# A two-layer decoder trunk on one core: the recurrent stage with a written order on ScalarE and VectorE

## The chip, the cores and the metric

The kernel runs on one core of a Trainium2 chip. Its engines are TensorE (PE, with weight loads shown as PEld), VectorE (DVE), ScalarE (ACT), GpSimd (POOL) and SyncE (SP), each with an instruction queue of its own; 16 DMA engines move data for all of them. The metric is the device time of the whole program in microseconds (us); lower is better.

## What is computed

Two layers work on x, 2048 tokens of 1024 channels in float32. Each normalises the rows, runs a mixer, normalises the result and adds it to x. The first mixer, a gated linear recurrence, is the stage that is changed; the second, a retention mixer, is not. Cut to what matters:

```python
def rglru_mixer(h, w_in, conv_w, conv_b, w_a, b_a, w_x, b_x, lam, w_out):
    u = h @ w_in                                  # 1024 -> 2 x 1536
    xb, gate = u[..., :D_RNN], u[..., D_RNN:]
    xb = causal_depthwise_conv(xb, conv_w, conv_b)   # 4 taps
    r = jax.nn.sigmoid(block_diagonal(xb, w_a) + b_a)   # 16 blocks of 96
    i = jax.nn.sigmoid(block_diagonal(xb, w_x) + b_x)
    log_a = -C_RG * r * jax.nn.softplus(-lam)
    a = jnp.exp(log_a)
    bt = jnp.sqrt(-jnp.expm1(2.0 * log_a)) * (i * xb)
    hseq = scan(h = a * h + bt)                   # along the tokens
    return (hseq * jax.nn.silu(gate)) @ w_out     # 1536 -> 1024

for layer in range(2):
    h = rms_norm(x, norm_pre[layer])
    o = rglru_mixer(h, ...) if layer == 0 else retention_mixer(h, ...)
    x = x + rms_norm(o, norm_post[layer])
```

## The kernel before

Every float32 product is made of three matmuls: each operand is split into a high part `hi` (ACT copies it into a shorter format) and the remainder `lo` (DVE subtracts), and `PASSES` multiplies hi by hi, hi by lo and lo by hi.

The recurrent stage has 16 steps. Step n works on channel group g = n // 4 (384 of the 1536 channels, three tiles of 128) and token block b = n % 4 (512 tokens). A step has two products of 72 matmuls each from x: `mm` gives the recurrent branch, `mg` the gate branch. Between them PE runs the 24 gate products `gt` of the step before (`Tail.products`, in four banks that sigmoids on ACT empty). x comes channel-major in four pieces of a token block. In g = 0 a piece is loaded raw (`xr<-xT`), multiplied by the norm's gain and split (`x_piece`), and stored by a GpSimd DMA to DRAM (`xs`); from g = 1 on it is read back whole (`xp<-xs`). Six weight tiles serve a group; spare buffers hold two more, the others are refilled as the products of b = 3 release theirs.

The norm's row factor is applied after the product: `row_stats` loads the token rows of a block (4 loads), squares them on ACT with a sum, takes a reciprocal root on DVE, and `row_scale` spreads it with four small products (`rbc`) into `sc`. DVE multiplies each product by `sc` (`rglru_u` for `mm`, `Tail.gate` for `mg`), runs the convolution (`Tail.conv`) and splits its result. The rows from 96 up of the three tiles go through a fourth tile `xd` (GpSimd DMAs); its gates `rd` come back by DMAs on ACT's queue into `ri`. The rest of a tail is `tanh`, `exp`, square root (ACT), and in `finish` the decay, the input term, the scan (DVE) and two multiplications on GpSimd, then a store to `y0`. Its ACT functions belong to four groups, so that ACT loads a table (`ACT_TABLE_LOAD`) four times in a step.

Then `out0` multiplies `y0` by the output weights (12 chunks, 72 matmuls for 128 tokens), the products named `o`; the first calls `upto(t, k)` take tokens 0 to 511 over the first chunks.

Order: PE's is the order of the program text. SP's loads and the ACT instructions marked with `keep_in_program_order` also keep it. All else on ACT, DVE and POOL is placed by a planner at compile time from its own costs, so that it can stand earlier or later than in the text. On the chip each engine runs its list in order, and an instruction that waits holds up all behind it. PSUM has eight banks, in turn for all products.

Of the kernel before, what the change touches and what calls it, by code (L numbers as in the profile page):

```python
# [65 lines left out]

class Kernel:
    def __init__(self, nc, tc, ctx, weights):
        self.nc, self.tc, self.ctx = nc, tc, ctx
        self.n = 0  # L70
# [31 lines left out]
    def tiny(self, s, n=1, bufs=4):  # L102
        return self.const.tile([P, n], F32, tag=f"{s}{n}", name=self.uid(s), bufs=bufs)
# [39 lines left out]
    def rsqrt(self, out, z, n=1):  # L143

        v = self.nc.vector
# [68 lines left out]
    def rglru(self, x, xT, gain, conv_w, conv_b, gate_w, b_a, b_x, lam, y0):  # L214


        nc = self.nc
        pool = self.p1 = Pool(self, "p1", (("c", (P, TB), F32, 18), ("ri", (P, 2 * TB), F32, 4),
                                           ("c2", (P, 2 * TB), F32R, 4),
                                           ("gw", (96, 768), F32R, 2), ("dg", (P, P), F32, 2), ("sc", (P, TB), F32, NB),  # L220
# [18 lines left out]
        w, xp = [], []  # L239
        for i in range(6):  # L240
# [4 lines left out]
            w.append(self.weight(shape=(P, KC, P), keep=False, ahead=0))  # L245
            if i < 4:
                xp.append(self.x_piece(0))
        stats = [self.row_stats(x, 0, "c2")]
        gw = gates(0)
        stats.append(self.row_stats(x, 1, "ri"))  # L250
        kt, ke = self.decay_coeffs(lam, pool)
        sc = [pool.tile("sc", (P, TB)) for _ in range(NB)]
        self.fetch_x(2)
        early, tail = [], None
        for n, (g, b) in enumerate(steps):
            final = n + 1 == len(steps)
# [11 lines left out]
            if n > 0:  # L268
                mg = self.rglru_gemm(w[3:], xp, False, (lambda: rows(2, 3)) if n == 1 else None)
            if final:  # L270
                px.close()
                self.py = Pool(self, "p2y", (("yp", (P, 1024), F32R, 8), ("yr", (P, 1024), F32, 2), ("pad", (P, 24), F32, 1)), "right")
                self.yraw = []
                self.ysrc = [(y0[b], 4 * m, o) for b in range(NB) for o in (0, 256) for m in range(3)]
# [16 lines left out]
            if tail:  # L291
                tail.exp()
                tail.finish()
            tail, xp = nxt, new
            if b == 3:
                early.append(self.weight())
                w = [[t.rearrange("p (k c) -> p k c", c=P) for t in e] for e in early]
            if n == 0:
                stats += [self.row_stats(x, i, "ri") for i in (2, 3)]
            if b == 0 and n > 0:  # L300
                gw = tail.gw = gates(g)

        self.fetch_y(2)
# [21 lines left out]
    def x_piece(self, ahead):  # L325
# [714 lines left out]
```

## Time and profile before

| | us |
|---|---|
| median of 3 runs (2703.66 to 2708.68) | 2705.45 |
| the profiled execution | 2711.98 |
| its span in the trace | 2710.2 |
| recurrent stage: first matmul to end of the last `mg` | 7.57 to 679.1 |

The profile is of one execution. Times in its rows count from the start of the span. Busy time is the time that an engine had an instruction in work; idle time is named with the instruction whose end released it. PEclk is the share of full speed that TensorE's clock was granted, 1.00 being 2.4 GHz and 0.50 being 1.2 GHz.

### The profile page before, as it was taken

What the parts mean: (1) busy time and instruction counts of PE and PEld (TensorE: products, weight loads), DVE (VectorE), ACT (ScalarE), POOL (GpSimd) and SP (SyncE); (2) the same over time, 40 slices, a digit from 0 to 9 for tenths busy, and PEclk for the clock granted to TensorE, in tenths of its full rate; (3) what the DMA queues carried; (4) which work ended last, traced back from release to release, by engine and by line L of the source; (5) the groups of instructions that cost most, each with busy time, mean ns of one, the idle gap of its engine ahead of it and who ended that gap; (6) DMA issues with size and microseconds to landing.
All of it is one profiled execution on the core that took longest, in us unless ns stands there. A gap on an engine that the chain in (4) does not pass through costs nothing.

```text
span 2710.2 us, 34140 instructions
## 1 busy us (share of the span) xinstructions
PE 2627.7 (97%) x13224; PEld 2219.1 (82%) x13224; DVE 1567.5 (58%) x3528; ACT 979.6 (36%) x1577; POOL 308.3 (11%) x298
## 2 busy tenths in 40 slices
PE   7889999999899999999999999999999999899998
PEld 6667878878688878888888888888888888778887
DVE  6677777678665555455654556545565456532332
ACT  5545555555432232223422234222342223311110
POOL 1233434345210000000000000000000000000000
PEclk9889999999899999999999999999999999999999
DMA  7554554554554451101411014110141101442231
GB/s 297 202 189 150 175 177 144 181 183 148 161 182 136 141 171 48 55 28 36 141 55 55 28 36 141 55 55 28 36 141 55 55 28 51 148 132 93 93 99 50
DMA packets 90723, 296.81 MB, mean 110 GB/s; under 512 B 10800, under 2 KB 31808, under 8 KB 82368
## 3 DMA queue, kind: packets, MB, share of 16 engines
q1 hardware_dynamic: 68128, 210.93, 24.3%
q0 software_dynamic: 19984, 77.13, 7.6%
q10 hardware_dynamic: 2448, 6.56, 1.0%
q8 instruction: 104, 1.70, 0.3%
q14 instruction: 59, 0.48, 0.1%
HBM read 210.69 MB, written 71.30 MB: 104 GB/s over the span
## 4 chain that ended last, share of the span: by engine, by line
PE 87%; DVE 5%; DMA 4%; ACT 3%; issue 1%; SPq 0%; DVEq 0%; ACTq 0%
PE o L94 26%; PE mm L94 14%; PE v L94 13%; PE g L94 12%; PE k L94 7%; PE q L94 7%; PE st L94 3%; PE gt L94 2%; DMA wraw<-w_in 2%; PE s L94 1%; PE y L97 1%; DVE w L123 1%; DMA wraw<-w_out 1%; DVE c L755 1%; DMA c<-x 1%
## 5 line engine op out<-in xcount | busy, mean ns | idle before, releaser
L94 PE MATMUL mm<-xp,w 128*128 128x512 f32 x2304 | 541.3, 396 | 23.9 <-ACT xp L339 7.6
L94 PEld LDWEIGHTS mm<-xp,w 128*128 128x128 f32 x2304 | 440.6, 192 | 121.6 <-ACT xp L339 7.6
L94 PE MATMUL o<-w,yp 128*128 128x512 f32 x1776 | 417.7, 395 | 10.9 <-ACT w L122 5.0
L94 PEld LDWEIGHTS o<-w,yp 128*128 128x128 f32 x1776 | 336.9, 191 | 83.8 <-ACT w L122 5.5
L94 PE MATMUL g<-w,hp 128*128 128x512 f32 x1536 | 363.6, 392 | 2.9 <-DVE w L123 2.9
L94 PE MATMUL v<-w,hp 128*128 128x512 f32 x1536 | 362.3, 395 | 4.1 <-DVE w L123 3.8
L94 PEld LDWEIGHTS v<-w,hp 128*128 128x128 f32 x1536 | 288.9, 190 | 64.7 <-DVE w L123 4.1
L94 PEld LDWEIGHTS g<-w,hp 128*128 128x128 f32 x1536 | 285.6, 188 | 62.5 <-DVE w L123 4.1
L915 DVE BATCH_NORM_STATS2 bst<-o 128x6 f32<-128x512 f32 x64 | 44.7, 699 | 304.8 <-PE o L94 304.7
L94 PE MATMUL q<-hp,w 128*128 128x256 f32 x1536 | 198.9, 286 | 0.0
L94 PE MATMUL k<-hp,w 128*128 128x256 f32 x1536 | 194.4, 283 | 0.0
L94 PEld LDWEIGHTS k<-hp,w 128*128 128x128 f32 x1536 | 190.7, 192 | 2.4
L94 PEld LDWEIGHTS q<-hp,w 128*128 128x128 f32 x1536 | 187.6, 191 | 0.1
L953 POOL DMA_DIRECT2D y<-m x32 | 21.6, 675 | 1325.7 <-ACT m L931 1325.7
L123 DVE TENSOR_TENSOR w<-wraw,w 128x1024 fp32r<-128x1024 f32 x89 | 114.9, 1301 | 77.7 <-ACT w L122 77.1
L94 PE MATMUL o<-w,w 128*128 128x512 f32 x624 | 144.9, 390 | 1.4 <-ACT w L122 0.9
L94 PEld LDWEIGHTS o<-w,w 128*128 128x128 f32 x624 | 116.9, 188 | 26.5 <-ACT w L122 1.4
L122 ACT ACTIVATE w<-wraw 128x1024 fp32r<-128x1024 f32 x89 | 92.7, 1053 | 114.4 <-DMA wraw<-w_in 88.2
L122 ACT ACTIVATE m<-m 128x128 fp32r<-128x128 f32 (+1 forms) x184 | 91.7, 515 | 112.3 <-DVE mv L916 97.6
L123 DVE TENSOR_TENSOR hp<-hr,hp 128x512 fp32r<-128x512 f32 x128 | 88.4, 693 | 62.2 <-ACT hp L122 40.0
L759 POOL TENSOR_TENSOR c<-c,c 128x512 f32<-128x512 f32 x48 | 91.1, 1902 | 267.4 <-DVE c L755 258.9
L94 PE MATMUL gt<-c,gw 96*96 96x512 f32 x384 | 97.9, 410 | 20.4 <-ACT ri L717 20.4
(179 smaller groups left out, 3324.8 us busy)
## 6 DMA issues: line engine op xcount, KB each, us to landing
xp<-xs SPq DMA_DIRECT2D x48, 1024.0 KB, 5.6
wraw<-w_in SPq DMA_DIRECT2D x66, 512.0 KB, 4.1
hr<-h1T SPq DMA_DIRECT2D x64, 512.0 KB, 4.8
yr<-y SPq DMA_DIRECT2D x52, 512.0 KB, 3.9
xs<-xp POOLq DMA_DIRECT2D x16, 1024.0 KB, 8.8
m<-x SPq DMA_DIRECT2D x32, 512.0 KB, 4.3
y<-m POOLq DMA_DIRECT2D x32, 512.0 KB, 6.1
y<-c POOLq DMA_DIRECT2D x48, 256.0 KB, 2.5
```

Of the source, the lines that this page charges most:

```text
L94: self.pe(self.nc.tensor.matmul(out, lhsT, rhs, start=start, stop=stop))
L97: self.pe(self.nc.tensor.transpose(out, src, self.ident))
L122: self.kept(self.nc.scalar.activation(hi, raw, AF.Copy), keep)
L123: self.kept(self.nc.vector.tensor_tensor(lo, raw, hi.bitcast(F32), ALU.subtract), keep)
L755: nc.vector.tensor_tensor_scan(h, e, s, 0.0 if b == 0 else k.last[j], ALU.mult, ALU.add)
L759: nc.gpsimd.tensor_tensor(sg, h, sg, ALU.mult)
L915: nc.vector.bn_stats(st, bo)
L953: self.nc.gpsimd.dma_start(y1[self.q][:, :, 4 * self.h : 4 * self.h + 4, :], self.sg.rearrange("p c (e t) -> p c e t", t=C))
```

## The change

`Ordered` wraps an engine so that all its instructions keep the order of the text. `va` (DVE) and `aa` (ACT) now issue nearly all of the recurrent stage; only `decay_coeffs` and POOL's instructions stay with the planner. The text is rearranged with it:

- start: the four pieces of the first block are stored by SP (`spill`), not by GpSimd: two behind the rows of block 1, two behind those of block 2. The rows of block 1 are loaded behind those of block 0 and the gate weights; those of blocks 2 and 3 in step 0. Rows 4 to 15 share one reciprocal root of 12 columns (`row_factor`), at the end of step 0. The `rbc` products are moved: block 0 to place 10 of 24 of the first `mg` (was 15), block 1 to place 19 of the second `mm`, blocks 2 and 3 to place 3 of the `mg` of steps 1 and 2.
- each step: the convolution, then its splits (`pieces`), then the weights, tanh, exp, decay, square root, scans with one x piece behind each, and only then the gate branch's `gate` and SiLU, which stood ahead of exp.
- weights: two at b = 1 (was b = 2), four at b = 3, whose raw tiles are all fetched by the end of b = 2 (`fetch(4, px, "xr")`).
- `products` takes the fourth tile first, and SP, not ACT, issues the three DMAs from `rd` to `ri`.
- end: the last `gt` stand behind the first 48 `o` products; in the last step the scans stand ahead of the splits of three of the eight output weights.

```diff
+class Ordered:
+
+    def __getattr__(self, name):
+        f = getattr(self.engine, name)
+
+        def call(*a, **kw):
+            ins = f(*a, **kw)
+            self.tc.keep_in_program_order(ins)
+            return ins
+
+        return call
...
-            self.split(gw[0], gw[1], raw)
+            self.split(gw[0], gw[1], raw, True)
...
-            w.append(self.weight(shape=(P, KC, P), keep=False, ahead=0))
+            w.append(self.weight(shape=(P, KC, P), keep=True, ahead=0))
             if i < 4:
-                xp.append(self.x_piece(0))
...
-        stats = [self.row_stats(x, 0, "c2")]
+                xp.append(self.x_piece(0, spill))
+        rs0, rest = self.tiny("rs", 4), self.tiny("rs", 12)
+        sq0, sqs = self.tiny("sq", 4), self.tiny("sq", 12)
+        stats = [(rs0, 0), (rest, 0), (rest, 4), (rest, 8)]
+        homes = [(self.wpool, "wraw")] * 2 + [(pool, "ri")] * 2
+        self.row_squares(x, 0, [(pool, "c2")] * 4, sq0, 0)
+        self.row_factor(sq0, rs0, 4)
         gw = gates(0)
-        stats.append(self.row_stats(x, 1, "ri"))
+        self.fetch_x(2)
+        self.row_squares(x, 1, homes, sqs, 0)
+        for dst, src in spill[:2]:
+            self.load(dst, src)
         kt, ke = self.decay_coeffs(lam, pool)
         sc = [pool.tile("sc", (P, TB)) for _ in range(NB)]
-        self.fetch_x(2)
...
-            def rows(*bs):
-                for i in bs:
-                    nc.scalar.activation(sc[i], self.row_scale(stats[i]), AF.Copy)
-
-            mm = self.rglru_gemm(w[:3], xp, n == 0, (lambda: rows(1)) if n == 1 else None)
+            def rows(i):
+                return lambda: aa.activation(sc[i], self.row_scale(*stats[i]), AF.Copy)
+
+            mm = self.rglru_gemm(w[:3], xp, n == 0, {19: rows(1)} if n == 1 else {})
             if n == 0:
-                mg = self.rglru_gemm(w[3:], xp, False, lambda: rows(0))
+                mg = self.rglru_gemm(w[3:], xp, False, {10: rows(0)})
             us = self.rglru_u(b, mm, sc[b])
             if tail:
                 tail.products()
             if n > 0:
-                mg = self.rglru_gemm(w[3:], xp, False, (lambda: rows(2, 3)) if n == 1 else None)
...
             nxt = Tail(self, g, b, gw, ba, bx, kt, ke, y0)
             if final:
                 break
             new = []
-            for j in range(3):
-                nxt.conv(j, us[j], cw, cb)
+            if b == 1:
+                self.fetch(2)
+            if n == 0:
+
+                self.row_squares(x, 2, homes, sqs, 4)
+                for dst, src in spill[2:]:
+                    self.load(dst, src)
                 new.append(self.x_piece(2))
-            if b == 2:
-                early = [self.weight() for _ in range(2)]
-            if b == 3:
-                early += [self.weight() for _ in range(3)]
-            if tail:
+                nxt.conv(0, us[0], cw, cb)
+                new.append(self.x_piece(2))
+                self.row_squares(x, 3, homes, sqs, 8)
+                new.append(self.x_piece(2))
+                nxt.gate(mg, sc[b])
+                nxt.conv(1, us[1], cw, cb)
+                new.append(self.x_piece(2))
+                nxt.conv(2, us[2], cw, cb)
+                self.row_factor(sqs, rest, 12)
+                nxt.pieces()
+                nxt.silu()
+            else:
+                for j in range(3):
+                    nxt.conv(j, us[j], cw, cb)
+                nxt.pieces()
+                if b == 1:
+                    early = [self.weight() for _ in range(2)]
+                if b == 3:
+                    early += [self.weight(ahead=0) for _ in range(2)]
                 tail.tanh()
-            new.append(self.x_piece(2))
-            nxt.gate(mg, sc[b])
-            nxt.silu()
-            if tail:
                 tail.exp()
-                tail.finish()
+                if b == 3:
+                    early.append(self.weight(ahead=0))
+                tail.decay()
+                new.append(self.x_piece(2))
+                tail.sqrt()
+                for j in range(3):
+                    tail.scan(j)
+                    new.append(self.x_piece(2))
+                if b == 3:
+                    early.append(self.weight(ahead=0))
+                nxt.gate(mg, sc[b])
+                nxt.silu()
+                if b == 2 and g + 1 < NG:
+                    self.fetch(4, px, "xr")
             tail, xp = nxt, new
             if b == 3:
-                early.append(self.weight())
                 w = [[t.rearrange("p (k c) -> p k c", c=P) for t in e] for e in early]
-            if n == 0:
-                stats += [self.row_stats(x, i, "ri") for i in (2, 3)]
             if b == 0 and n > 0:
                 gw = tail.gw = gates(g)
...
         for j in range(3):
             nxt.conv(j, us[j], cw, cb)
+        nxt.pieces()
+        early += [self.weight() for _ in range(2)]
         tail.tanh()
+        tail.exp()
+        self.pcs = [[self.y_piece(True)]]
+        early.append(self.weight())
+        tail.decay()
+        tail.sqrt()
+        self.pcs[0].append(self.y_piece(True))
+        for j in range(3):
+            tail.scan(j)
         early += [self.weight() for _ in range(2)]
-        tail.exp()
-        tail.finish()
-        self.pcs = [[self.y_piece() for _ in range(2)]]
-        early += [self.weight()]
-        nxt.products()
         nxt.gate(mg, sc[b])
-        self.pcs[0].append(self.y_piece())
-        early += [self.weight() for _ in range(3)]
+        early.append(self.weight())
+        self.pcs[0].append(self.y_piece(True))
         return early, nxt
...
-            self.nc.scalar.activation(hi[:, c], raw[:, c], AF.Copy, scale=gk)
-            self.nc.vector.scalar_tensor_tensor(lo[:, c], raw[:, c], gk, hi[:, c].bitcast(F32), ALU.mult, ALU.subtract)
-        self.nc.gpsimd.dma_start(self.xs[b][j], both.bitcast(F32))
+            self.aa.activation(hi[:, c], raw[:, c], AF.Copy, scale=gk)
+        for c in range(2):
+            k = 2 * j + c
+            gk = self.gain[:, k : k + 1]
+            self.va.scalar_tensor_tensor(lo[:, c], raw[:, c], gk, hi[:, c].bitcast(F32), ALU.mult, ALU.subtract)
+        if later is None:
+            self.nc.gpsimd.dma_start(self.xs[b][j], both.bitcast(F32))
+        else:
+            later.append((self.xs[b][j], both.bitcast(F32)))
         self.fetch_x(ahead)
...
+    def row_squares(self, x, b, homes, sq, at):
+
+        for i, (pool, tag) in enumerate(homes):
+            xn = pool.tile(tag, (P, D))
             self.load(xn, x[b * TB + i * P : b * TB + (i + 1) * P, :])
+            self.aa.activation(xn, xn, AF.Square, accum_out=sq[:, at + i : at + i + 1])
+
+    def row_factor(self, sq, rs, n):
+
+        z = self.tiny("z", n)
+        self.va.tensor_scalar(z, sq, 1.0 / D, RMS_EPS, ALU.mult, ALU.add)
+        self.rsqrt(rs, z, n, self.va)
...
-            if m == 15 and between:
-                between()
+            if m in between:
+                between[m]()
...
+        upto(0, 8)
+        tail.products()
         tail.tanh()
         tail.exp()
+        self.pcs.append([self.y_piece(True)])
+        tail.decay()
+        tail.sqrt()
         tail.silu()
-        self.pcs.append([self.y_piece()])
-        tail.finish()
-        upto(0, 8)
+        for j in range(3):
+            tail.scan(j)
...
+    def pieces(self):
+
+        k = self.k
+        for j in range(3):
+            vp = self.pool.tile("c2", (P, 2, TB), F32R)
+            k.split(vp[:, 0], vp[:, 1], self.xc[j], True)
+            self.nc.gpsimd.dma_start(self.xd[32 * j : 32 * j + 32].bitcast(F32), vp[96:128].bitcast(F32))
+            self.xcp.append(vp)
...
-        for j in range(4):
+        for i, j in enumerate((3, 0, 1, 2)):
             src = self.xd if j == 3 else self.xcp[j][:96]
             dst = rd if j == 3 else ri[j][:96]
             for e, bias in ((0, self.ba), (1, self.bx)):
...
-                self.k.tc.keep_in_program_order(nc.scalar.activation(dst[:, e, :], o, AF.Sigmoid, bias=bias[:, 4 * self.g + j : 4 * self.g + j + 1]))
-        for j in range(3):
-            nc.scalar.dma_start(ri[j][96:128], rd[32 * j : 32 * j + 32])
+                k.aa.activation(dst[:, e, :], o, AF.Sigmoid, bias=bias[:, 4 * self.g + j : 4 * self.g + j + 1])
+            if j == 3:
+                for m in range(3):
+                    k.load(ri[m][96:128], rd[32 * m : 32 * m + 32])
...
+    def decay(self):
+
         for j in range(3):
-            self.k.tc.keep_in_program_order(nc.scalar.activation(self.ri[j][:, 0, :], self.tt[j], AF.Sqrt))
-
-    def finish(self):
+            h, e = self.tt[j], self.ee[j]
+            i = self.ri[j][:, 1, :]
+            self.nc.gpsimd.tensor_tensor(i, i, self.xc[j], ALU.mult)
+            self.k.va.scalar_tensor_tensor(e, e, 1.0, h, ALU.add, ALU.mult)
+            self.k.va.tensor_scalar(e, e, -1.0, 1.0, ALU.mult, ALU.add)
+
+    def sqrt(self):
+        for j in range(3):
+            self.k.aa.activation(self.ri[j][:, 0, :], self.tt[j], AF.Sqrt)
```

## Rows read from the trace of the kernel before

**Rows 1.** the page's busy time of each engine, whole span

```profile
PE 2627.7 (97%) x13224; PEld 2219.1 (82%) x13224; DVE 1567.5 (58%) x3528; ACT 979.6 (36%) x1577; POOL 308.3 (11%) x298
```

**Rows 2.** the chain that ended last, an undisturbed stretch: start, us, what

```profile
263.58 5.55 PE gt L94 x24
269.14 32.66 PE mm L94 x144
```

**Rows 3.** steps b=2,3,0,0: busy us (count) of PE, PEld, DVE, ACT, POOL; clock, DMA

```profile
301.80:340.00 38.20, 38.20 (x169) 30.89 (x169) 29.46 (x47) 21.65 (x29) 17.07 (x12) 1.00 0.53 180
...
340.00:379.30 39.30, 38.33 (x169) 30.68 (x168) 24.97 (x35) 21.96 (x30) 9.83 (x11) 1.00 0.55 187
...
379.30:423.00 43.70, 40.60 (x170) 32.02 (x169) 38.06 (x57) 21.61 (x30) 16.23 (x14) 0.96 0.45 151
...
537.50:581.00 43.50, 40.42 (x170) 31.89 (x169) 38.06 (x57) 21.52 (x30) 16.42 (x14) 0.96 0.48 152
```

**Rows 4.** PE in order of time: start, us, instruction, [idle before, releaser]

```profile
84.44 2.88 PE L94 MATMUL gt<-c,gw 96*96 96x512 f32 x6 [9.47 <-ACT ri L717]
...
177.98 2.88 PE L94 MATMUL gt<-c,gw 96*96 96x512 f32 x6 [8.89 <-ACT ri L717]
...
217.07 5.90 PE L94 MATMUL mm<-xp,w 128*128 128x512 f32 x18 [3.40 <-DMA xp<-xs]
...
232.46 7.77 PE L94 MATMUL mm<-xp,w 128*128 128x512 f32 x33 [2.02 <-DVE w L123]
...
707.58 1.22 PE L94 MATMUL o<-w,yp 128*128 128x512 f32 x2 [5.02 <-ACT w L122]
```

**Rows 5.** busy times of longer stretches, columns as in rows 3

```profile
72.03:90.34 18.31, 8.49 (x26) 5.11 (x24) 12.39 (x41) 13.96 (x25) 0.50 (x1) 0.64 0.65 234
...
90.34:127.93 37.59, 37.03 (x161) 30.30 (x160) 22.15 (x41) 21.04 (x31) 9.33 (x10) 0.95 0.53 185
...
166.14:183.75 17.61, 8.50 (x26) 5.13 (x25) 11.40 (x19) 13.50 (x18) 1.86 (x2) 0.68 0.14 50
...
183.75:222.81 39.06, 35.66 (x145) 28.90 (x144) 26.80 (x38) 20.46 (x27) 10.27 (x10) 0.92 0.57 182
...
222.81:263.58 40.77, 38.75 (x170) 30.85 (x169) 36.55 (x54) 20.32 (x29) 16.00 (x13) 1.00 0.49 162
...
679.10:709.60 30.50, 19.92 (x69) 13.42 (x67) 20.91 (x21) 15.15 (x20) 9.99 (x8) 0.81 0.51 145
...
709.60:757.00 47.40, 47.40 (x198) 38.96 (x199) 32.36 (x60) 20.58 (x30) 9.86 (x9) 0.94 0.51 172
```

**Rows 6.** groups of instructions on DVE and POOL: busy, mean ns, idle before

```profile
L697 DVE SCALAR_TENSOR_TENSOR c<-u,c_cw,c 128x512 f32<-128x512 f32 x144 | 103.9, 775 | 0.0
...
L755 DVE TENSOR_TENSOR_SCAN c<-c,last,ri 128x512 f32<-128x512 f32 x36 | 53.3, 1500 | 0.0
...
L123 DVE TENSOR_TENSOR w<-wraw,w 128x1024 fp32r<-128x1024 f32 x89 | 114.9, 1301 | 77.7 <-ACT w L122 77.1
...
L154 DVE TENSOR_TENSOR rst<-rst,rsz 128x4 f32<-128x4 f32 x12 | 1.9, 162 | 0.4
...
L391 DVE COPY u<-halo 128x3 f32<-128x3 f32 x36 | 27.5, 763 | 0.0
...
L750 POOL TENSOR_TENSOR ri<-ri,c 128x512 f32<-128x512 f32 x48 | 102.5, 2160 | 71.5 <-DMA ri<-ri 63.9 <-issue 7.7
```

**Rows 7.** ACT in order of time, the end of one switch of functions

```profile
175.95 1.28 ACT L717 ACT_TABLE_LOAD   x1
...
177.25 0.68 ACT L717 ACTIVATE ri<-gt,c_ba 96x512 f32<-96x512 f32 x1
```

**Rows 8.** DMA issues (KB, us to landing); busy times of two stretches

```profile
c<-x SPq DMA_DIRECT2D x4, 512.0 KB, 19.1
...
20.00:25.00 5.00, 5.00 (x24) 4.13 (x23) 2.56 (x9) 1.27 (x2) 0.47 (x1) 1.00 1.02 425
...
30.00:35.00 5.00, 5.00 (x24) 4.14 (x23) 0.00 (x0) 3.03 (x5) 0.00 (x0) 1.00 1.04 331
```

More of the change, by code (lines that the diff above doesn't have):

```diff
@@ L102, in tiny @@
     def tiny(self, s, n=1, bufs=4):
-        return self.const.tile([P, n], F32, tag=f"{s}{n}", name=self.uid(s), bufs=bufs)
+        return self.const.tile([P, n], F32, tag=f"{s}{n}", name=self.uid(s), bufs=bufs if n < 12 else 1)
     def bank(self, shape, s="ps"):
@@ L141, in weight, with rsqrt @@
         return hi, lo
-    def rsqrt(self, out, z, n=1):
-        v = self.nc.vector
+    def rsqrt(self, out, z, n=1, v=None):
+        v = v or self.nc.vector
         y, t, zh = self.tiny("rsy", n), self.tiny("rst", n), self.tiny("rsz", n)
@@ L268, in rglru @@
             if n > 0:
-                mg = self.rglru_gemm(w[3:], xp, False, (lambda: rows(2, 3)) if n == 1 else None)
[L270 to L274, printed above, removed]
+                mg = self.rglru_gemm(w[3:], xp, False, {3: rows(n + 1)} if n in (1, 2) else {})
             nxt = Tail(self, g, b, gw, ba, bx, kt, ke, y0)
@@ L300, in rglru @@
             if b == 0 and n > 0:
                 gw = tail.gw = gates(g)
+        px.close()
+        self.py = Pool(self, "p2y", (("yp", (P, 1024), F32R, 8), ("yr", (P, 1024), F32, 2), ("pad", (P, 24), F32, 1)), "right")
+        self.yraw = []
+        self.ysrc = [(y0[b], 4 * m, o) for b in range(NB) for o in (0, 256) for m in range(3)]
         self.fetch_y(2)
@@ L323, in fetch_x, with x_piece @@
             self.xraw.append(raw)
-    def x_piece(self, ahead):
+    def x_piece(self, ahead, later=None):
         g, b, j = self.xnext.pop(0)
@@ L362, in row_scale, with rglru_gemm @@
             dg = self.p1.tile("dg", (P, P))
-            nc.vector.tensor_scalar(dg, self.ident, rs[:, i : i + 1], None, ALU.mult)
+            self.va.tensor_scalar(dg, self.ident, rs[:, at + i : at + i + 1], None, ALU.mult)
             self.mm(rbc[:, i * P : (i + 1) * P], self.ones, dg, start=True, stop=True)
         return rbc
-    def rglru_gemm(self, tiles, xp, arrival=False, between=None):
+    def rglru_gemm(self, tiles, xp, arrival=False, between={}):
         out = [self.bank([P, TB], "mm") for _ in tiles]
@@ L381, in rglru_u @@
     def rglru_u(self, b, mm, scale):
-        nc = self.nc
+        v = self.va
         us = []
@@ L451, in fetch_y, with y_piece @@
             self.yraw.append(raw)
-    def y_piece(self):
+    def y_piece(self, keep=False):
         self.fetch_y(2)
         hi, lo = [self.py.tile("yp", (P, 4, 256), F32R) for _ in range(2)]
-        self.split(hi, lo, self.yraw.pop(0))
+        self.split(hi, lo, self.yraw.pop(0), keep)
         self.fetch_y(2)
@@ L690, in conv @@
     def conv(self, j, u, cw, cb):
[L692 to L695 removed]
+        k, ch = self.k, 3 * self.g + j
+        v = self.pool.tile("c", (P, TB))
+        k.va.tensor_scalar(v, u[:, :TB], cw[:, ch, 0:1], cb[:, ch : ch + 1], ALU.mult, ALU.add)
         for t in range(1, CW):
[L697 to L700 removed]
+            k.va.scalar_tensor_tensor(v, u[:, t : t + TB], cw[:, ch, t : t + 1], v, ALU.mult, ALU.add)
         self.xc.append(v)
[L702 removed]
+    def pieces(self):
[5 more added lines that the diff above has]
+            self.xcp.append(vp)
     def products(self):
@@ new lines, in decay, with scan @@
+            h, e = self.tt[j], self.ee[j]
[6 more added lines that the diff above has]
+            self.k.aa.activation(self.ri[j][:, 0, :], self.tt[j], AF.Sqrt)
+    def scan(self, j):
+        nc, k, b = self.nc, self.k, self.b
+        s, i, h, e, sg = self.ri[j][:, 0, :], self.ri[j][:, 1, :], self.tt[j], self.ee[j], self.sg[j]
+        k.va.scalar_tensor_tensor(s, e, 1.0, s, ALU.add, ALU.mult)
+        k.va.tensor_tensor(s, s, i, ALU.mult)
+        k.va.tensor_tensor_scan(h, e, s, 0.0 if b == 0 else k.last[j], ALU.mult, ALU.add)
+        if b < NB - 1:
+            k.last[j] = k.tiny("last", 1, 6)
+            k.va.tensor_copy(k.last[j], h[:, TB - 1 : TB])
+        nc.gpsimd.tensor_tensor(sg, h, sg, ALU.mult)
+        nc.gpsimd.dma_start(self.y0[b][3 * self.g + j], sg)
```

62 lines of the change are left out of this document (16 added, 46 removed).

## The prediction

> **What bounds the kernel now.** I read the page first. PE is busy for 97% of the span [rows 1], so time can come back only where PE stands or runs at half clock. The chain of waits then gives the floor. In an undisturbed stretch 24 gate products take 5.55 us and 144 branch products 32.66 [rows 2], so a step of the recurrent stage cannot take less than 38.21 us, and one matmul of 512 columns costs 0.227 us. In such a step PE is busy from end to end and DVE for 29.46 us of it [rows 3]: DVE is the next limit, with 8.7 us to spare.
>
> The busy times by stretch show where steps take longer. From the first matmul to the end of the last `mg` 671.5 us pass, where 32 branch products of 16.33 and 15 sets of gates need 605.8. The 66 us over it stand in four places, and a fifth lies behind them.
>
> - Steps 0 to 2, up to 127.93: 120.4 us for five branch products and one set of gates, 87.2. PE stands 9.47 us for a sigmoid queued behind squares of late rows [rows 4], and the gates that follow run at 0.48 us each, half clock [rows 5, 4].
> - Step 3, 166.14 to 222.81: 56.67 us for one step, 18.46 lost. Gates wait 8.89 us for sigmoids that stand on ACT behind a tail whose weights came late; later `mm` waits 3.40 us for an x piece that SP issued behind weight loads [rows 4]. Step 4 loses 40.77 - 38.21 = 2.56 [rows 5], 2.02 of it for the low part of a weight [rows 4].
> - Steps 7 and 8: 39.30 + 43.70 - 76.42 = 6.6 lost [rows 3].
> - Steps 11 and 12 repeat this; the second takes 43.50, 5.3 lost [rows 3].
> - The head of the output product, 679.10 to 757.00: 77.9 us for 24 gates and 240 `o` products, 5.55 + 54.4 = 60.0, so 17.9 lost. 5.02 is a wait for a weight [rows 4]; the clock was 0.81 and 0.94 [rows 5].
>
> **The change part by part.**
>
> *Steps with b = 3.* Today the weights for the next group are fetched by SP between x pieces, so a step 7 leaves DVE idle (24.97 us busy) and step 8 overfull (38.06) [rows 3]. The change fetches all raw tiles a step ahead and splits two weights before tanh, one behind exp, one behind the scans. DVE's work in such a step is the 29.46 of a step with two splits plus two more at 1.23 (1.30 in the mean [rows 6]), 32 us. In the written order DVE waits only for exp, some 3 us, and ends near 35 to 36. Behind it stand SiLU and a table load of 1.28 [rows 7] before the next sigmoids at 38.2 + 0.7. That fits by about 1.5 us. So I recover 17.5 of the 18.46, 2 of the 2.56, 6 of the 6.6 and 4.5 of the 5.3. If the fit fails, each us beyond it costs one per b = 3 step.
>
> The gate's move behind the scans costs nothing while the next gates need only two of its three banks after 2.8 us; it hides behind the 32.66 us of branch products.
>
> *The three DMAs from `rd`* move from ACT to SP and past no queue of loads that waits later than they do: the x loads ahead of them were released when the `mg` before ended, 16 us earlier. The fourth tile's sigmoids come first, so they issue sooner. No gain is counted.
>
> One rule of the Trainium skill weighs against a chain with four switches of function: ScalarE: Activation LUTs, section What ACT_TABLE_LOAD costs, gives 1283 ns for the load and about 1380 ns of draining with it. By it the fit of 1.5 us would be nearly gone and the two switches ahead of the last scans would cost 2.8: a sum smaller by about 4, 2672. The trace has 1.28 us and the sigmoid 0.02 behind [rows 7], so I go by the row.
>
> *The start.* Rows of block 0 take 19.1 us to land behind 4 MB of stores that GpSimd interleaves, with the DMA engines at 1.0 [rows 8]. Deferring the stores leaves 7.3 MB ahead of their end. At 331 to 425 GB/s [rows 8] that is 21 to 25 us instead of 34, and the first `rbc` no longer waits: PE ends step 0 near 43 instead of 48. I take 360, nearer to the lower, in whose stretch GpSimd issues no store.
>
> Then the written order costs. Gate weights, two x pieces, the rows of block 1, two stores and the rows of block 2 make 15.0 MB: block 2 lands near 44, and the first x piece of step 1 stands behind its squares on ACT, so `mm` starts at 46. Behind two more stores and two x pieces block 3 lands near 59 (20.2 MB). Its squares end at 60; behind them stand x piece 3, the gate, two convolutions, x piece 4, the 12-column root (eleven instructions of 0.16 with a start every 0.2 [rows 6]), three low parts and four diagonals: 1.4 + 2.0 + 2.6 + 1.4 + 2.6 + 2.2 + 1.9 + 1.1 = 15.2, at 0.65 to 0.75 for each pass over 512 columns [rows 6]. So the root's `rbc` in the second `mm` can go at 76, after PE has stood since 68. Five places of three matmuls are left, 3.4 us at full and 6.8 at half clock; `mm` ends near 83 (72.03 now), the gates near 88.5, and the second `mg` starts there against 90.34 [rows 5]. Step 1's rest takes 32.7 + 1.4 + 1, to 123.2 instead of 127.93; step 2 pays one more `rbc` (1.4) and 0.7 of DVE pressure: 163.6 instead of 166.14. Gain 2.5. Bounds: if nothing but DMA bounded this part, `mm` would end near 64, 19 us better; if block 3 lands 10 us later, it is 8 us worse than now.
>
> *The end.* PE no longer waits for `gt`'s sigmoids first: 48 `o` products stand ahead. But three output weights are split behind the last scans. Counted from the end of `mg`, DVE does the splits before at about 0, then decay 3, a y piece 1.3, three scans with two multiplications each 8 (scan 1.50 [rows 6]), two weights 2.5, the gate 2; the last weight's load starts when a raw tile frees, at 13, takes some 5 and is split by 20. Work for PE until then is 10.9 us, so 9.5 are lost, with about 3 at half clock after the wait. 12.5 replace 17.9: gain 5. Bounds: 12 if the weights come with the scans, 0 if the last load is 5 us later.
>
> Sum: 2.5 + 17.5 + 2 + 6 + 4.5 + 5 = 37.5 us. The profiled execution took 2711.98, its span 2710.2; it lies 0.24% above the median of 2705.45, so I take the difference from the median: 2668. Past 757.00 nothing is changed, and I expect the same time there.
>
> **The rivals.**
>
> *The start comes out dense.* If block 3's rows land by 50, the chain on DVE is the only limit, step 1 ends 15 to 19 us sooner: 2650. For it: the DMA engines move up to 425 GB/s. Against: the rows are issued behind x loads that wait for DVE.
>
> *The start comes out later.* Rows of block 3 at 70 push everything by 10, since block 1's factor, which needed no other block before, waits for all twelve columns: 2680, with 2 of it hidden. For it: one root for three blocks. Against: fewer stores compete.
>
> *Nothing to win.* If the waits at b = 3 are the DMA engines' own and not the order's, they stay: 2705, within 0.2%. Against: the 3.40 us wait was for an x piece that SP issued late, while DMA share in step 7 is 0.55 [rows 3].
>
> *Slower: DVE and GpSimd cannot run together.* In the 29.46 us step POOL is busy for 17.07, some 13.8 without its six DMA issues. If DVE's back-to-back order leaves POOL no gap, and the two exclude each other, a step takes 29.5 + 13.8 = 43.3, 5.1 over the floor; over 15 steps that is 76 us, less the 37.5: 2744. It decides from 40.7 us of joint work in a step (2.5 over the floor, 15 times). For it: a copy of three columns takes 0.76 us in the mean and POOL's multiplication 2.16 [rows 6], so one does hold up the other. Against: the step of [rows 3] holds 29.46 + 13.8 in 38.20, so the durations already contain the waiting. A milder form, with only the four b = 3 and the two x-splitting steps over, gives +15 and 2683.
>
> The Trainium skill, SBUF — State Buffer, section Who interferes with whom, states that rule: the shared port pair is an exclusive lock, held for a whole instruction. By it 43.3 would be the step; the trace has 38.20.
>
> **How the numbers follow.** My forecast 0.53; dense start 0.14 (2650); later start 0.12 (2680); milder lock 0.10 (2683); nothing won 0.06 (2705); full lock 0.05 (2744). 0.2% is 5.4 us, about what a measurement of this kernel can tell from no change. Faster is everything but the last two: 0.89; within 0.06; slower 0.05. The forecast's own range is 2657 to 2679 from the bounds of its terms. To leave out no more than 2 in 10 I go from 2648, which takes in the dense start, to 2692, which takes in the later start and the milder lock.
>
> **What would show it.** Right: steps 4 to 15 at 38.2 to 39 us with no gap at b = 3 above 1 us; sigmoids never released by DVE's gate; gates near 83 to 89 with PE idle before the `rbc` of the second `mm`; 166.14 becoming about 164 and 222.81 about 203; the output head with one gap on a weight near 9 us. Wrong: a sigmoid of each step released late by SiLU; DVE past 38 us in a step; x or row loads behind stores on SP in step 0; the output weights late beyond 20 us after the last `mg`.

## The result and the profile after

The changed kernel takes 2730.3 us (median of 4 runs, 2723.2 to 2731.1) against 2705.6 before: ratio 1.0084, 95% interval 1.0065 to 1.0104. It is 24.7 us slower, where I had forecast 37.5 faster. The profiled execution has a span of 2729.3 us, 19.1 above that of before, which lay above its own median.

The page's busy times, as in [rows 1]:

```profile
PE 2646.1 (97%) x13224; PEld 2215.4 (81%) x13224; DVE 1598.5 (59%) x3504; ACT 975.0 (36%) x1577; POOL 254.9 (9%) x294
```

PE has the same 13,224 matmuls and stands about as long (83.2 us idle, 82.5 before), but is busy for 18.4 us more. The busy times by stretch, columns as in [rows 3], of steps 6, 8 and 9 and of the output head:

```profile
295.00:334.00 39.00, 39.00 (x170) 31.00 (x169) 30.66 (x45) 19.54 (x27) 11.71 (x12) 1.00 0.51 176
...
373.00:413.40 40.40, 39.27 (x170) 30.95 (x169) 33.12 (x50) 21.33 (x31) 12.56 (x12) 1.00 0.48 156
413.40:456.70 43.30, 41.02 (x170) 31.93 (x169) 32.75 (x48) 22.10 (x30) 11.51 (x12) 0.96 0.52 183
...
679.76:765.80 86.04, 67.44 (x267) 51.16 (x265) 57.15 (x89) 38.46 (x54) 17.93 (x17) 0.90 0.45 147
```

The first is a step without any gap, at a granted clock of 1.00, and takes 39.00 us where [rows 3] has 38.20. So the floor itself moved. PE's instructions in order of time, with what ended the wait before them, can be held against [rows 4]:

```profile
64.61 8.22 PE L112 MATMUL mm<-xp,w 128*128 128x512 f32 x21 [10.77 <-ACT xp L77]
78.96 2.08 PE L112 MATMUL rbc<-dg,ones 128*128 128x128 f32 x8 [6.13 <-DVE dg L77]
...
215.84 3.87 PE L112 MATMUL gt<-c,gw 96*96 96x512 f32 x12 [2.38 <-ACT ri L77]
...
438.33 18.52 PE L112 MATMUL mm<-xp,w 128*128 128x512 f32 x72 [2.24 <-DMA xp<-xs]
...
698.03 4.58 PE L112 MATMUL o<-w,yp 128*128 128x512 f32 x10 [10.64 <-DVE w L141]
...
739.29 4.43 PE L112 MATMUL o<-w,yp 128*128 128x512 f32 x10 [5.48 <-DVE w L141]
```

The waits of 9.47 and 8.89 us for sigmoids are gone. In step 1's first product PE now waits for an x piece and then for the diagonals; `rbc` starts at 78.96, where I had 76. The new waits that were not forecast stand at the gates behind a step with b = 3, at an x piece a step later, and at the second place in the head. The groups on DVE and POOL, columns as in [rows 6] (line 77 is the wrapper that issues all ordered instructions):

```profile
L77 DVE SCALAR_TENSOR_TENSOR c<-u,c_cw,c 128x512 f32<-128x512 f32 x144 | 138.8, 964 | 5.1
...
L77 DVE SCALAR_TENSOR_TENSOR ri<-c,ri 128x512 f32<-128x512 f32 x48 | 54.0, 1126 | 0.0
L77 DVE TENSOR_TENSOR_SCAN c<-c,last,ri 128x512 f32<-128x512 f32 x36 | 46.2, 1284 | 1.3
...
L77 DVE COPY u<-halo 128x3 f32<-128x3 f32 x36 | 5.7, 158 | 0.0
...
L815 POOL TENSOR_TENSOR ri<-ri,c 128x512 f32<-128x512 f32 x48 | 74.4, 1573 | 173.1 <-DMA ri<-ri 115.6 <-ACT ri L77 57.4
```

Before, the scan's first multiplication was

```profile
L753 DVE SCALAR_TENSOR_TENSOR ri<-c,ri 128x512 f32<-128x512 f32 x48 | 32.8, 686 | 8.5 <-ACT ri L743 8.5
```

A convolution's multiply-add takes 964 ns (775 before), the scan's first multiplication 1126 (686 before), while the halo copy fell from 763 to 158 and POOL's multiplication from 2160 to 1573. DVE and POOL in order of time show why:

```profile
278.78 1.81 DVE L77 SCALAR_TENSOR_TENSOR ri<-c,ri 128x512 f32<-128x512 f32 x1
280.70 0.69 DVE L77 TENSOR_TENSOR ri<-ri 128x512 f32<-128x512 f32 x1
...
286.74 1.89 DVE L77 TENSOR_TENSOR c<-mm,sc 128x512 f32<-128x512 f32 x3
...
278.75 1.29 POOL L833 TENSOR_TENSOR c<-c,c 128x512 f32<-128x512 f32 x1 [9.81 <-DVE c L77]
...
286.72 1.29 POOL L833 TENSOR_TENSOR c<-c,c 128x512 f32<-128x512 f32 x1 [1.82 <-DVE c L77]
```

At 278.75 POOL starts to multiply; the DVE instruction issued 0.03 us later takes 1.81 us instead of 0.69. At 286.72 POOL starts again, and three DVE multiplications with one operand in PSUM take 1.89 us together, against 1.87 at 372.47, where POOL does not multiply. The end of step 7, a step with b = 3, on DVE and then on ACT:

```profile
372.47 1.87 DVE L77 TENSOR_TENSOR c<-mm,sc 128x512 f32<-128x512 f32 x3
...
375.02 1.28 ACT L77 ACT_TABLE_LOAD   x1
376.32 0.68 ACT L77 ACTIVATE ri<-gt,c_ba 96x512 f32<-96x512 f32 x1
```

DVE ends the gate at 374.3, 40.3 us after the first gate product of the step. The last SiLU, a table load and only then the sigmoid follow, and the `gt` that started at 372.99 wait 1.13 us for it.

By stretches of the spans (the first two columns are what I forecast and had; the last two are experiments):

| us | forecast | before | changed | e1: place restored | e7: and multiplications on DVE |
|---|---|---|---|---|---|
| to the gates of step 3 | 163.6 | 166.1 | 171.5 | 172.3 | 163.9 |
| step 3 | 39.2 | 56.7 | 39.0 | 38.2 | 38.2 |
| steps 4 to 15, to the last `mg` | 443.8 | 456.3 | 469.2 | 467.7 | 443.0 |
| head, to the first transposes | 72.7 | 77.7 | 85.9 | 84.9 | 88.1 |
| all behind it | 1953.4 | 1953.4 | 1963.6 | 1952.0 | 1953.3 |

### The profile page after: what moved, and what is told of

Read it like the earlier page. It is cut to its first block, busy times and chain, and to the rows that moved or that the text cites. A ratio compares the mean times of both kernels' runs of the same rounds, so it can differ in the third digit from the quotient of the medians.

```text
span 2729.3 us, 34188 instructions
## 1 busy us (share of the span) xinstructions
PE 2646.1 (97%) x13224; PEld 2215.4 (81%) x13224; DVE 1598.5 (59%) x3504; ACT 975.0 (36%) x1577; POOL 254.9 (9%) x294
## 4 chain that ended last, share of the span: by engine, by line
PE 80%; DVE 11%; ACT 3%; DMA 3%; issue 2%; SPq 0%; DVEq 0%; ACTq 0%
PE o L112 26%; PE v L112 13%; PE g L112 12%; PE mm L112 9%; PE k L112 7%; PE q L112 7%; DVE c L77 6%; PE st L112 3%; DVE ri L77 1%; ACT c L77 1%; PE s L112 1%; PE y L115 1%; DVE w L141 1%; PE gt L112 1%; ACT w L140 1%
## 5 line engine op out<-in xcount | busy, mean ns | idle before, releaser
L112 PE MATMUL mm<-xp,w 128*128 128x512 f32 x2304 | 553.5, 401 | 28.6 <-ACT xp L77 18.4
L112 PEld LDWEIGHTS mm<-xp,w 128*128 128x128 f32 x2304 | 440.7, 192 | 137.6 <-ACT xp L77 19.1
L112 PE MATMUL o<-w,yp 128*128 128x512 f32 x1776 | 427.0, 399 | 20.4 <-DVE w L141 17.7
L77 DVE SCALAR_TENSOR_TENSOR c<-u,c_cw,c 128x512 f32<-128x512 f32 x144 | 138.8, 964 | 5.1
L141 DVE TENSOR_TENSOR w<-wraw,w 128x1024 fp32r<-128x1024 f32 x83 | 102.4, 1247 | 45.5 <-ACT w L140 45.0
L473 ACT ACTIVATE m<-o 128x512 f32<-128x512 f32 x62 | 37.0, 597 | 234.0 <-PE o L112 156.0
```

The lines of the kernel that those rows point to most:

```text
L77: ins = f(*a, **kw)
L112: self.pe(self.nc.tensor.matmul(out, lhsT, rhs, start=start, stop=stop))
L141: self.kept(self.nc.vector.tensor_tensor(lo, raw, hi.bitcast(F32), ALU.subtract), keep)
L473: self.kept(nc.scalar.activation(res[:, 512 * i : 512 * i + 512], o[i], AF.Square, accum_out=sq[:, i : i + 1]), keep)
```

## The experiments

**Where the operands lie: e1, e2, e3.** The new 12-column scalars made the constant pool 384 bytes larger by my count of its tiles; no trace shows addresses. All pools filled from the left, the weights among them, moved up by 384 bytes; those filled from the right, with x and y pieces, did not. In the changed kernel the slow products are those with one operand on each side.

```diff
 e1, changed kernel, wpool:      ("pad", (P, 24), F32, 1)  ->  ("pad", (P, 56), F32, 1)
 e2, kernel before, wpool:       ("pad", (P, 24), F32, 1)  ->  ("pad", (P, 120), F32, 1)
 e3, changed kernel, p1x, p2y:   ("pad", (P, 24), F32, 1)  ->  ("pad", (P, 56), F32, 1)
```

> The changed kernel with 128 bytes more of padding ahead of its weights; nothing else differs. The changed kernel's constant pool is 384 bytes larger than before's, so every pool that is filled from the left moved by 384 bytes, and those filled from the right did not; this pad takes the weights back to the place that they had before within a block of 512 bytes. Theory A (a matmul whose two operands lie differently within such a block is slower): 144 branch products take 32.66 us again in place of 33.46, `o` products 0.227 us each in place of 0.232, PE busy goes from 2646 back to about 2628, and the time from 2730 to about 2705 to 2710. Rival B (the order of the work, not the place of its operands, slows PE or makes the whole loss): matmuls stay at 0.2324 us and the time at 2730, within 3 us.

> The kernel before with 384 bytes more of padding ahead of its weights; no instruction and no order differs. Theory A: its branch products take 33.46 us for 144 in place of 32.66, `gt`, `q`, `k`, `g` and `v` keep their rates, PE is busy for about 2646 us, and the time is 2720 to 2730. Rival B: 2705, and 32.66 us for 144.

> The changed kernel with 128 bytes more of padding at the right end of the two pools that hold the x pieces and the y pieces, which moves these pieces 128 bytes down; the weights stay where they slowed. Theory A in its relative form (what counts is how the two operands lie to each other): 32.66 us for 144 products again, and about 2705 to 2712. In its absolute form (the weights' own place counts): 33.46 us, and 2730. Rival B: 2730 and 33.46 us as well.

Measured: e1 2716.2 us (ratio to before 1.0042, 1.0028 to 1.0056), e2 2722.1 (1.0061, 1.0046 to 1.0076), e3 2717.7 in one run. The groups on PE (busy, mean ns; idle and its releasers), first of the changed kernel, then of e1, e2 and e3:

```profile
L112 PE MATMUL mm<-xp,w 128*128 128x512 f32 x2304 | 553.5, 401 | 28.6 <-ACT xp L77 18.4 <-DVE xp L77 4.0 <-DMA xp<-xs 3.9
```

```profile
L112 PE MATMUL mm<-xp,w 128*128 128x512 f32 x2304 | 542.9, 396 | 32.2 <-ACT xp L77 19.5 <-DMA xp<-xs 7.7 <-DVE xp L77 5.0
```

```profile
L94 PE MATMUL mm<-xp,w 128*128 128x512 f32 x2304 | 553.1, 401 | 20.5 <-ACT xp L339 8.1 <-DVE w L123 6.0 <-DVE xp L340 3.7
```

```profile
L112 PE MATMUL mm<-xp,w 128*128 128x512 f32 x2304 | 540.8, 396 | 30.3 <-ACT xp L77 18.3 <-DVE xp L77 4.7 <-DMA xp<-xs 4.4
...
L112 PE MATMUL o<-m,yp 128*128 128x512 f32 x144 | 35.0, 395 | 0.0
```

Theory A holds in its relative form. The kernel before, with not one instruction changed, gets the slow rate from 384 bytes of padding and loses 16.3 us. Moving either operand of the changed kernel by 128 bytes more gives the fast one, with 14.1 us gained in e1; e3's last line is of a later product whose y pool was not moved, and it stays at 35.0 (34.1 in e1, 34.1 before). So weights and pieces that have moved against each other by 0 or by 512 bytes are fast, by 384 slow; other distances were not tried, and with what period the rate returns is not shown. This is 14 of the 24.7 us, and e1 still loses 10.4.

**The x loads behind the weights: e4.** In e1, steps 5, 9 and 13 take 42.7 to 43.0 us. SP's queue and PE in one of them:

```profile
259.88 11.63 SPq L118 DMA_DIRECT2D wraw<-w_in  x4
...
271.57 5.63 SPq L118 DMA_DIRECT2D xp<-xs  x4
...
279.21 18.17 PE L112 MATMUL mm<-xp,w 128*128 128x512 f32 x72 [2.36 <-DMA xp<-xs]
```

```diff
-                    early = [self.weight() for _ in range(2)]
+                    early = [self.weight(ahead=0) for _ in range(2)]
...
                     tail.scan(j)
                     new.append(self.x_piece(2))
+                if b == 1:
+                    self.fetch(2)
```

> On the changed kernel with the 128 bytes of padding (2716.2 us): in the steps with b = 1 the third and fourth raw weight are fetched behind the four x loads instead of ahead of them; no other order changes. Theory C (x loads stand on SP behind two weight loads, which wait for the raw tiles that DVE frees at the low parts of the early weights): the waits of `mm` for an x piece, 2.36, 2.78 and 2.54 us, go, and so does the slower half step behind each, 17.98 to 18.21 us for 72 products in place of 16.4; each of the three steps takes 38.2 us in place of 42.7 to 43.0, and the time falls by 10 to 14, to about 2704. Rival (the DMA engines are busy in that stretch, and the piece lands late anyway): the waits stay within 1 us and the time within 3.

2703.9 us (0.9991, 0.9981 to 1.0001): 12.3 less than e1, as theory C says, and the three waits are gone. The loads did stand behind two weight loads, and those behind DVE's split of the weights. That DVE was late for a reason of its own is seen in e7, where the same waits all but vanish (0.33 us left) without this edit.

**SiLU behind the sigmoids: e5.**

```diff
                 tail.products()
+                if b == 0:
+                    tail.silu()
...
                 nxt.gate(mg, sc[b])
-                nxt.silu()
+                if b < 3:
+                    nxt.silu()
```

> On the same base (2716.2 us): after a step with b = 3 the three SiLUs run behind the sigmoids of the next step instead of ahead of them. Theory D (the gates of that step wait for sigmoids that stand on ACT behind SiLU and a table load, and these behind the gate on DVE, whose work in such a step ends at 40 us): the three waits of `gt` for ACT, 3.06, 1.92 and 1.91 us, go, with the half-clock gates behind them, and the time falls by 8 to 11, to about 2706. Rival (the late place of DVE itself counts, and something else on DVE is late next, the low parts of x or the scales): another wait of 2 to 3 us takes their place, and the time stays within 3 us of 2716.

2710.5 us (1.0018, 1.0008 to 1.0027), 5.7 less, between theory and rival. The gates wait no more (0.21 us left), but part of the gain went back, as the rival said: PE now waits 3.31, 3.99 and 4.52 us for the x piece, 2.36, 2.78 and 2.54 in e1.

```profile
432.65 19.18 PE L112 MATMUL mm<-xp,w 128*128 128x512 f32 x72 [3.99 <-DMA xp<-xs]
```

**The old head: e6.** `tail.products()` stands ahead of `upto(0, 8)` again, and the scans ahead of the last weights and y pieces:

```diff
         for j in range(3):
             tail.scan(j)
-        early += [self.weight() for _ in range(2)]
+        self.pcs = [[self.y_piece(True) for _ in range(2)]]
+        early.append(self.weight())
+        nxt.products()
         nxt.gate(mg, sc[b])
...
```

> On the same base (2716.2 us): the end part alone is undone; the last gate products go ahead of the first output ones again, and the last scans of the tail ahead of the splits of the last output weights. Theory E (the two weights split behind the scans cost more than the cover of 32 products gives): the waits for weights in the head, 11.0 and 5.0 us, become about 5 and 3, and the time falls by about 7, to 2709. Rival (the head is bound by the serial chain of two tails, whatever their order): within 2 us of 2716.

2717.1 us (1.0041, 1.0026 to 1.0056), 0.9 more than e1: the rival. The waits moved: gates 2.96 us, then 4.63 for a weight. The sigmoids of the last tail end at 689.8, but its tanh starts at 706.4, behind two weight copies on ACT that wait for raw tiles, so its scans and the weights behind them are no earlier. So the order of the products alone was not what cost.

**POOL's multiplications on DVE: e7 and e8.** The same two edits, in the changed kernel with e1's padding and (with `nc.vector` for `va`) in the kernel before:

```diff
-            self.nc.gpsimd.tensor_tensor(i, i, self.xc[j], ALU.mult)
+            self.k.va.tensor_tensor(i, i, self.xc[j], ALU.mult)
...
-        nc.gpsimd.tensor_tensor(sg, h, sg, ALU.mult)
+        k.va.tensor_tensor(sg, h, sg, ALU.mult)
```

> On the same base (2716.2 us): both multiplications of a tail that GpSimd does (`ri` by `c`, and `h` by the gate) are done by VectorE, six instructions more a step on DVE and none on POOL but DMA issues. Theory F (a DVE instruction that runs beside a POOL multiplication is held up for about as long as that one runs): a convolution's multiply-add falls from 0.96 us to 0.775 in the mean, the scan's two multiplications from 1.13 and 0.86 to 0.69, and the six new ones cost 0.69 each; DVE is busy for the same time within 1 us a step, and the waits of the steps behind b = 3 stay as they are or shrink: 2710 to 2718. Rival (the durations have another cause, such as PE or ACT reading beside it): durations stay, DVE has 4.1 us more a step, and the steps with b = 3 grow by some 4 us each: 2728 or more.

> The kernel before, with the two multiplications of a tail on VectorE instead of GpSimd; its order and its addresses stay. If the lock between DVE and POOL is what made the written order lose, and the order itself is worth something once the lock is gone: before gains little from this, since its losses in the recurrent stage stand at late weights and squares (9.47, 8.89 and 3.40 us) and not at DVE: 2698 to 2706, well behind the 2688 of the changed kernel with the same edit. Rival (the 28 us came from the lock alone and the written order adds nothing): 2680 to 2690, the same as the changed kernel with that edit.

e7 takes 2688.0 us (0.9935, 0.992 to 0.995): 28.2 less than e1, far below the range I gave. e8 takes 2701.2 (0.9978, 0.9968 to 0.9988), as expected. Groups on DVE in e7, then its step 7 by stretch, the gate on DVE that ends it, and the gate products that follow without a wait:

```profile
L77 DVE SCALAR_TENSOR_TENSOR c<-u,c_cw,c 128x512 f32<-128x512 f32 x144 | 108.3, 752 | 5.1
...
L77 DVE SCALAR_TENSOR_TENSOR ri<-c,ri 128x512 f32<-128x512 f32 x48 | 32.9, 685 | 0.0
...
L77 DVE TENSOR_TENSOR ri<-ri,c 128x512 f32<-128x512 f32 x48 | 32.9, 684 | 0.0
```

```profile
317.00:355.20 38.20, 38.20 (x169) 30.90 (x168) 32.88 (x53) 22.11 (x30) 3.17 (x6) 1.00 0.46 152
```

```profile
352.66 1.88 DVE L77 TENSOR_TENSOR c<-mm,sc 128x512 f32<-128x512 f32 x3
```

```profile
355.22 5.71 PE L112 MATMUL gt<-c,gw 96*96 96x512 f32 x24
```

DVE does 96 multiplications more, some 65.7 us at 0.684, and is busy for 1574.9 us instead of 1598.3: it had been held for 65.7 + 23.4 = 89 us. It was not waiting for POOL's results: in the changed kernel no idle time of PE, DVE or ACT ends on a POOL multiplication. The Trainium skill, SBUF — State Buffer, section Who interferes with whom, says that DVE and GpSimd share a port pair that is locked for a whole instruction, and that a DVE instruction with at most one SBUF input stays out of it unless it runs in a two-port mode; the 1.81 us beside POOL, and the 1.89 for three with a PSUM operand, agree. The first instruction of a convolution, with one SBUF tensor, was held too (784 ns in the mean against 541 in e7); no run here shows its mode.

The kernel before was held about as long: 1567.5 - (1550.3 - 65.6) = 83 us. There it cost only 4.9 us: PE's waits for DVE's splits of weights and x in the recurrent stage (6.0 and 3.8 us) are still there in e8 (6.3 and 3.8). Put together (the changed order with e1's padding):

| us | order of before | written order |
|---|---|---|
| multiplications on POOL | 2705.8 | 2716.2 |
| multiplications on DVE | 2701.2 | 2688.0 |

The written order is worth -13.2 us with the lock gone and +10.4 with it.

**A new head: e9.** On e7, whose head takes 88.1 us:

```diff
-        upto(0, 8)
-        tail.products()
         tail.tanh()
         tail.exp()
-        self.pcs.append([self.y_piece(True)])
-        tail.decay()
         tail.sqrt()
         tail.silu()
-        for j in range(3):
-            tail.scan(j)
+        tail.decay()
+        w.append(self.weight())
+        tail.scan(0)
+        w.append(self.weight())
+        tail.scan(1)
+        tail.scan(2)
+        self.pcs.append([self.y_piece(True)])
+        upto(0, 6)
+        upto(1, 6)
+        upto(0, 8)
         upto(1, 8)
```

and ahead of it, as in e6, scans and `products` before the last weights.

> On the kernel with the multiplications on VectorE (2688.0 us), whose output head takes 88 us from the last `mg` to the first transposes: the scans of the last tail but one and the last gate products go first again, the tanh, exp, sqrt and SiLU of the last tail stand ahead of the last two weights on ACT, its scans between their splits on DVE, and the first two output tiles use six weights each before either waits for the seventh. Theory E2 (the head is the serial chain of two tails, and it stretched because ACT and DVE waited for the raw tiles of the last weights in between): the two waits for weights, 8.8 and 8.1 us, fall to under 3 together, the head takes about 70 us, and the time is about 2670 to 2675. Rival (the DMA of the weights is the limit, whatever the order): the waits return at the seventh and ninth weight with 10 us or more, and the time is 2684 to 2690.

2671.6 us (0.9864, 0.9844 to 0.9884), 16.4 less than e7. The head by stretch, and its longest waits for a weight and a y piece:

```profile
648.50:722.50 74.00, 64.11 (x265) 49.50 (x264) 53.85 (x95) 36.81 (x52) 4.38 (x8) 0.98 0.51 163
```

```profile
680.50 4.16 PE L112 MATMUL o<-w,yp 128*128 128x512 f32 x17 [2.85 <-DVE w L141]
688.38 34.31 PE L112 MATMUL o<-w,yp 128*128 128x512 f32 x143 [3.72 <-DVE yp L141]
```

So the weights' DMA did not bound the head at 88 us. e9 moves the products, the last tail on ACT and DVE, the splits and the places of the `o` products together; e6, with the multiplications still on POOL, says that the products and scans moved without the last tail give nothing. Which share each of the others has was not tried.

**The start: e10, e11, e12.** One root for each block again, and the late rows behind the x pieces; in e10 the core of the edit is

```diff
-                self.row_squares(x, 2, homes, sqs, 4)
...
                 new.append(self.x_piece(2))
-                self.row_squares(x, 3, homes, sqs, 8)
+                xn = self.row_loads(x, 2, homes)
+                nxt.conv(1, us[1], cw, cb)
                 new.append(self.x_piece(2))
...
+                self.row_squares(xn, sqs[2])
+                self.row_factor(sqs[2], rss[2], 4)
                 nxt.silu()
```

with block 3 in step 1 in the same way. It also issues all four stores of the first block behind the rows of block 1 and moves the `rbc` of blocks 2 and 3 from place 3 to 12. No scalar has 12 columns any more, so these kernels need no padding for the fast rate. e11 is e10 with e9's head. e12 is e11 with the x pieces of step 1 put between its convolutions and its weights last.

> On the kernel with the multiplications on VectorE (2688.0 us), start part: each block of rows has its own root again, the rows of block 2 are loaded behind two x loads and squared behind all four x pieces of step 1, the rows of block 3 a step later behind the sigmoids. Theory G (the wait of 10.97 us for ACT is x behind squares of late rows, and the one of 6.90 for the diagonals is the root over twelve columns): both go or fall under 3 us, the first gates start near 72 us in place of 84.3, and the time is about 2675 to 2680. Rival (DMA traffic bounds the start, and the x pieces are late whatever stands ahead of them on ACT): the second `mm` starts at 62 or later, and the time is 2685 to 2690.

> Both edits of the two kernels before this one together, on the kernel with the multiplications on VectorE. By theories E2 and G: about 2660 (2688 less some 16 for the head and 11 for the start). By both rivals: 2684 to 2690.

> On the kernel with the multiplications on VectorE and the new head (2671.6 us), a second form of the start. The first form took the wait of 10.97 us away (gates at 72.5 us instead of 84.3) but lost more in the next step: the x pieces of step 2 stood on ACT behind rows, weights, tanh and exp, and `mm` waited 11.39 us for them. Now the four x pieces of step 2 go between the convolutions and the tail, the last rows are squared between them and behind the scans, the weights of that step come last, and the root of block 2 stands behind the diagonals of block 1. Theory G2 (the order on ACT, and not DMA, bounds the second step too): gates near 70 to 72 us, the step behind them 39 to 42 us instead of 56.5, and the time about 2656 to 2660. Rival (the raw x tiles come late from memory in that stretch, whatever stands ahead of them): the wait for x moves behind DMA, the step still takes 50 us or more, and the time is 2668 or more.

None gained: e10 takes 2693.0 us (5.0 above e7), e11 2682.5 and e12 2676.9 (10.9 and 5.3 above e9; ratio of e12 0.989, 0.9873 to 0.9906, which overlaps that of e9). PE in e10, then in e12:

```profile
72.53 5.97 PE L112 MATMUL gt<-c,gw 96*96 96x512 f32 x24
...
107.13 0.79 PE L112 MATMUL mm<-xp,w 128*128 128x512 f32 x1 [11.39 <-ACT xp L77]
```

```profile
67.25 6.01 PE L112 MATMUL gt<-c,gw 96*96 96x512 f32 x24 [1.34 <-DMA c<-c]
...
118.99 2.88 PE L112 MATMUL gt<-c,gw 96*96 96x512 f32 x6 [7.90 <-DVE c L77]
...
151.10 14.55 PE L112 MATMUL mm<-xp,w 128*128 128x512 f32 x54 [2.83 <-DVE xp L77]
```

Each form starts the gates earlier than e7 (84.3), as theory G has it, and gives all of it back later: in e10 step 1 takes 56.5 us (40.4 in e7), in e12 it takes 42.3 but step 2 takes 60.4 (39.1 in e7). Rows, x pieces, weights and a tail share ACT, DVE and a few raw tiles, and whichever is put last is the next wait. What a start without loss would need was not found; e9 is the fastest kernel, 1.36% below before.

## Why the prediction was wrong

- **The floor.** "What bounds the kernel now" took 0.227 us for a matmul as given. The change moved weights against x and y by 384 bytes, and each such product costs 0.232: 14.1 us (e1), 11.6 of them behind the head, in products that the diff does not touch. In the recurrent stage the 10.6 us more of `mm` (553.5 against 542.9) mostly shortened waits that were there anyhow. No row of before could show it, but the diff did show larger constants.
- **Steps with b = 3.** "That fits by about 1.5 us" is the step that failed. I had DVE at its end 35 to 36 us after the step's first gates; it ended after 40.3 (374.3), and the gates waited. The rival of a full lock was the right mechanism with the wrong size and argument. I set it aside because a step of before holds DVE and POOL together in 38.20 us, "so the durations already contain the waiting". They do, but on whichever instruction meets POOL. Before, 21.8 of some 83 us fell on halo copies (27.5 us against 5.7 in the changed kernel); in the written order the held time fell on the chain from convolution to gate, SiLU and the next sigmoids, and on the splits that free raw tiles. A busy total of 29 to 33 us does not show that the chain ends at 40. From e1 to e7 the held time is worth 28.2 us. Without it DVE still ends 37.5 us after the first gates (354.5 in e7), some 2 later than I had it. No gate waits there, but the sum of DVE's work was too short, and that the fit holds in e7 is partly luck. That the full lock's 2744 lies nearer to the result than my 2668 is luck as well, since 14 of the 24.7 us have another cause.
- **SP's queue.** I priced the earlier fetches of raw weights at nothing. With DVE late they stood ahead of the x loads and held them up: 12.3 us (e4), a part of those 28.
- **The terms of the recurrent stage** were right otherwise. With both costs taken out (e7) the gates of step 3 start at 163.9 (forecast 163.6), step 3 takes 38.2 (39.2), the rest of the stage 443.0 (443.8).
- **The head.** Forecast to gain 5, it loses 7.2 in e1 and 10.4 in e7. The eighth weight came about as late as I had worked out (22 us behind the last `mg` in e7, forecast 20). What I left out is what the late gates push: `gt` at 668.4 is 23 us behind `mg`, and the last scans, and the ninth weight behind them on DVE, follow; PE waits 8.1 us more at 704.4. In e9, with that tail ahead of the last weights, the head takes 14.1 us less.
- **The table load** went as the row said: the sigmoid after the gate comes 0.02 us behind a load of 1.28, and no drain shows.

Of the miss of 62, 14 are the place of the operands, 28 the lock, 15 the head. The rest, some 5, I put down to the start of the sum: I took the gains, found in an execution 6.5 us above the median, off the median. Against that execution e7's span is 23.7 us less, and the forecast terms with the head as measured give 22.1.

## What to carry to other kernels

When an edit changes the size of any small tile, compare the rate of an undisturbed product before and after at the same granted clock; if it differs, pad the pool before judging the order. Before writing out an order for DVE, find which of its instructions run beside GpSimd's and price the chain with each of those held for a whole GpSimd instruction, or take the work off GpSimd first: here that turned the written order from a loss of 10 us into a gain of 13, each against the old order with its multiplications on the same engine. A stage whose loads, splits and tail share engines hands a removed wait on to the next step, so look two steps further before counting it.

## What the runs showed of the hardware

- At a granted clock of 1.00 a matmul of 512 columns costs 0.2325 us (32.08 us for 138) when the tiles of its two operands have moved against each other by 384 bytes, against 0.2268 with 0 or 512; products with both operands in pools that moved together (`gt`, 5.55 us for 24) did not change.
- A DVE multiplication of two SBUF tensors issued 0.03 us behind a POOL multiplication took 1.81 us instead of 0.69; three with a PSUM operand each were not held (1.89 us beside POOL, 1.87 without).
- Moving 96 multiplications of 128x512 from POOL to DVE made DVE busy for 23.4 us less, not more.
